# One layer of a hybrid encoder on one core: token groups of 4, 4, 3, 3, 3 tiles in place of 3, 4, 4, 3, 3

## The chip, the core and the metric

The kernel runs on one core of a Trainium2 chip. The metric is the device time of one execution in microseconds (us), as a median of several runs. The core has five engines with a queue each: PE (TensorE, matrix multiplies; its weight loads are listed as PEld), DVE (VectorE), ACT (ScalarE), POOL (GpSimd) and SP (SyncE, which here only issues transfers). An instruction waits at the head of its engine's queue until what it reads is there and what it overwrites has been used; all behind it wait too. Transfers (DMAs) are issued from SP's and ACT's queues.

## The reference

One layer is computed for 2048 new frames of one stream and 16 further frames of 8 running streams, all in float32, with 1024 channels. Cut to what matters:

```python
h = rmsnorm(x, norm_mix_pre)
P = h @ w_in            # q|k|v (3*512) | z 512 | b 4 | a 4 | B 512 | C 512 | H 512
qkv, conv_new = causal_dwconv(qkv_in, conv_prev, conv_qkv_w)   # 4 taps, then SiLU
q, k = l2norm(q) * 128 ** -0.5, l2norm(k)                      # 4 heads of 128
beta, g = sigmoid(b_raw), -exp(a_log) * softplus(a_raw + dt_bias)
o, S_new = gated_delta_rule(q, k, v, g, beta, S0, chunk)       # has a triangular solve per chunk
o = rmsnorm(o, gdn_norm_w) * silu(z)
sc_y, sc_new = causal_dwconv(sc_c * sc_h, sc_prev, conv_sc_w)  # 3 taps
x = x + rmsnorm(concat([o, sc_b * sc_y]) @ w_o, norm_mix_post)
h = rmsnorm(x, norm_ffn_pre)
x = x + rmsnorm((silu(h @ w_gate) * (h @ w_up)) @ w_down, norm_ffn_post)
```

The outputs are the new x of both streams, the last rows of both convolutions and the states S. The inputs come from one seed; some gains are multiplied by constant factors.

## The kernel before, in words

The 2176 rows are 17 tiles of 128 (tile 16 holds the running streams). Every large product is made exact enough by splitting each operand into a rounded part (`hi`, `wh`: made by a cast on ACT) and the rest (`lo`, `wl`: made by a subtraction on DVE), and by adding three products, `wh*hi + wh*lo + wl*hi`.

The kernel has four stages: the input projection with the delta rule (up to about 904 us), the output projection, the gated feed-forward part, and its way back. The change touches only the first.

**Groups and blocks.** The tiles are worked on in groups (`GROUPS`, L31). A group of n tiles is n*128 columns wide, and all 28 blocks of 128 columns of `w_in` are multiplied with it, each in 24 multiplies (8 slices of the depth, three products each, L298). `BLOCKS` names them: 0 to 3 k, 4 to 7 v, 8 to 11 q, 12 to 15 z, and from 16 on C, H, B of the short convolution. `SEQS` gives the order, one for the first group (group 0) and one for the others. Each block's weights are brought by `fetch` and `weights`, ahead of use: three buffers `w2` for the split pair, two `wr` for the raw weights. Group 0 loads raw weights (512 KB), splits them on ACT and DVE (L277, L278) and stores the pair (`wsplit`, 1024 KB) so that later groups load it ready; every fourth block is stored only in group 1. `stores` keeps a store back until the next block's load has been issued. In group 0 the rows are not yet normalised when they are multiplied; a factor per column, `rb`, is applied when a bank is taken out of PSUM (L309 and others, on DVE). In later groups the rows are scaled beforehand (`x_norm`, `x_split`).

**The written order.** PE's order is written out by hand (`tc.manual_schedule` for PE); the other engines' orders are made by a planner that simulates the program, with `tc.issue_after(i)` keeping an instruction behind `i` on the same engine. Each block takes three steps (depth slices 0 to 2, 3 to 5, 6 and 7, so 9, 9 and 6 multiplies), 84 steps a group; behind each step the functions that `events` holds for it are traced. `plan` puts them there: `PLAN` has, by number of tiles (0 stands for group 0), the steps of the gates' rates, their sums, the decays, the mask, the key norms, the key pairs, the loading of the triangular solve, its storing, the four levels that join its 32-wide answers to 128-wide ones, and the first chunk of the recurrence (a chunk a tile, six steps apart). What goes beyond step 83 runs in the next group. The solve (L578, L580) is 31 pairs of short instructions on DVE. Also in `plan`: the next group's rows are loaded and squared (`x_rows_load`, `x_rows`), their factors made and broadcast by a multiply with ones (`x_spread`, which calls `spread`: DVE sum, POOL power, DVE diagonal, PE broadcast), the transposed rows loaded, scaled and split.

**The start.** The slices of group 0 are loaded and split (L215, L216), the first block is multiplied slice by slice, then the second and third; then PE sums the squares of the rows (L888, one-column multiplies), multiplies the gates' small weights (`gate_matmuls`), and broadcasts the factors (`spread`). The fourth block can start when a PSUM bank of the first three has been taken out. Nine small inputs and constants are issued on ACT's queue after the split of the last slice (`inputs`, `late`).

Of the kernel before, what the change touches and what calls it, by code (L numbers as in the profile page):

```python
# [17 lines left out]
P = 128  # L18
D = 1024
# [11 lines left out]
GROUPS = [[0, 1, 2], [3, 4, 5, 6], [7, 8, 9, 10], [11, 12, 16], [13, 14, 15]]  # L31
# [53 lines left out]
def kernel(  # L85
# [6 lines left out]
    w_ba,  # L92
# [3 lines left out]
    conv_w,  # L96
    sc_w,
# [5 lines left out]
    gates,  # L103
    gsc,
# [25 lines left out]
    cst = const.tile([P, 904], F32, name="cst")  # L130
    half_eye = consts[:, 904:]
    nc.scalar.dma_start(out=cst[:, 0:256], in_=consts[:, 0:256])
    late = lambda: nc.scalar.dma_start(out=cst[:, 256:], in_=consts[:, 256:904])
    ident, ones, tri_p, tri_s, blk_s, smask, neg_p, neg_s = (cst[:, a:b] for a, b in CONSTS.values())
    vec = const.tile([P, 17], F32, name="vec")
    nc.scalar.dma_start(out=vec, in_=vecs)
    g_pre = vec[:, 0:8]
# [20 lines left out]
    with ExitStack() as ph:  # L158
# [18 lines left out]
        junko = gp.tile([P, P], BF16, name="junko")  # L177
        half = gp.tile([P, 4 * MAXT], F32, name="half")
# [22 lines left out]
        def spread(r, n):  # L201
            c = n * P
            rg = xbuf()
            V.tensor_mul(rg[:, :c].rearrange("p (t i) -> p t i", t=n), ident.unsqueeze(1).broadcast_to([P, n, P]),
                         r.unsqueeze(2).broadcast_to([P, n, P]))
            ps = tbank()
            T.matmul(ps[:, :c], ones, rg[:, :c], start=True, stop=True)
# [13 lines left out]
        def x_rows_load(tiles, i, nx):  # L221
            if not i:
                nx["ss"] = small.tile([P, 2 * MAXT], F32, tag="xss", name="xss")
            nx["xt"] = []
# [12 lines left out]
        def x_spread(tiles, nx):  # L237
            n = len(tiles)
            ss = nx["ss"]
            V.tensor_add(ss[:, :n], ss[:, :n], ss[:, MAXT:MAXT + n])  # L240
            nx["rb"] = spread(rstd(small, ss[:, :n], n, 1.0 / D, EPS, "x"), n)
            nx["hi"], nx["lo"], nx["xk"] = [], [], []
# [20 lines left out]
        def weights(j, gi):  # L263
# [10 lines left out]
            for q in range(parts):  # L274
                c = slice(KD // parts * q, KD // parts * (q + 1))
                wload = nc.sync.dma_start(out=wr[:, c], in_=w_in[j, :, c])
                A.copy(wh[:, c], wr[:, c])  # L277
                V.tensor_tensor(out=wl[:, c], in0=wr[:, c], in1=wh[:, c].bitcast(F32), op=ALU.subtract)  # L278
            wloads.append(wload)
            while stores:  # L280
                stores.pop()()
# [150 lines left out]
        def gate_matmuls(hi, lo, n):  # L432
            ps = bank()
            mm3(ps[:16, :n * P], [(wba[:, k, :], v[k][:, :n * P]) for k in range(KD) for v in (hi, lo)])
            return ps
# [119 lines left out]
        def solve_load(g):  # L555
# [3 lines left out]
            nc.sync.dma_start(out=Ts, in_=half_eye)  # L559
# [222 lines left out]
        def plan(g, nx, events):  # L782
# [10 lines left out]
            rates, sums, decay, mask, norms, pairs, load, store, levels, chunks = PLAN[n if gi else 0]  # L793
# [26 lines left out]
            if nx is not None:  # L820
# [5 lines left out]
                at(48 + 3 * m, x_spread, tiles, nx)  # L826
                ts = [62, 65, 68, 69, 70, 71, 72, 73]
                for k in range(KD):
                    at(ts[k], x_load, tiles, k, nx)
                    if k < NHX:  # L830
                        at(ts[k] + 3, x_norm, tiles, k, nx)
                        at(ts[k] + 4, x_split, tiles, k, nx)
                    else:
                        at(ts[k] + 4, x_norm, tiles, k, nx)
# [36 lines left out]
        for k, raw in enumerate(raws):  # L871
            sq = xbuf()
            if k % 2:
                V.tensor_mul(sq[:, :c], raw, raw)
                V.tensor_add(sq[:, :c], sq[:, :c], sqs[-1][:, :c])
                sqs[-1] = sq
            else:
                A.activation(sq[:, :c], raw, AF.Square)
# [12 lines left out]
        started = mark["hi"].ins  # L891
        inputs = ExitStack()
        inputs.enter_context(tc.issue_after(started))
        late()
        cw = gp.tile([P, 12, 4], F32, name="cw")
        scw = gp.tile([P, 4, 3], F32, name="scw")
        nc.scalar.dma_start(out=cw, in_=conv_w)
        nc.scalar.dma_start(out=scw, in_=sc_w)
        cch = gp.tile([P, 12, NS, 3], F32, name="cch")
        sch = gp.tile([P, 4, NS, 2], F32, name="sch")  # L900
        nc.scalar.dma_start(out=cch, in_=cache_c)
        nc.scalar.dma_start(out=sch, in_=cache_s)
# [4 lines left out]
        al = gp.tile([P, 4], F32, name="al")  # L907
        nega = gp.tile([P, 4], F32, name="nega")
        nc.scalar.dma_start(out=al, in_=gates[0].partition_broadcast(P))
        A.activation(nega, al, AF.Exp)  # L910
        V.tensor_scalar_mul(nega, nega, -1.0)
        gsct = gp.tile([16, 1], F32, name="gsct")
        nc.scalar.dma_start(out=gsct, in_=gsc)
        gbia = gp.tile([16, 1], F32, name="gbia")
        V.memset(gbia, 0.0)
        nc.scalar.dma_start(out=gbia[4:8, :], in_=gates[1].unsqueeze(1))
        wba_r = gp.tile([P, KD, 8], F32, name="wba_r")
        nc.scalar.dma_start(out=wba_r, in_=w_ba)
        inputs.close()
        wba = gp.tile([P, KD, 16], F32R, name="wba")  # L920
        A.copy(wba[:, :, 0:8], wba_r)
        V.tensor_sub(wba[:, :, 8:16], wba_r, wba[:, :, 0:8].bitcast(F32))
        gps = gate_matmuls(hi, lo, n)
        rb = spread(rx, n)
# [4 lines left out]
        events = {}  # L929
        for gi, tiles in enumerate(GROUPS):  # L930
            g = new_group(gi, hi, lo, rb)
# [592 lines left out]
def pack(i):  # L1524
# [13 lines left out]
    a["w_ba"] = w[:, 2048:2056].reshape(KD, P, 8).transpose(1, 0, 2)  # L1538
# [4 lines left out]
    a["conv_w"] = f["conv_qkv_w"][0].reshape(4, 12, P).transpose(2, 1, 0)  # L1543
    a["sc_w"] = f["conv_sc_w"][0].reshape(3, 4, P).transpose(2, 1, 0)
# [4 lines left out]
                                f["gdn_norm_w"][0].reshape(1, P).T], axis=1)  # L1549
    a["rows"] = np.concatenate([f["norm_mix_post"], f["norm_ffn_post"]])  # L1550
    a["gates"] = np.concatenate([f["a_log"], f["dt_bias"]])
    a["gsc"] = np.array(([-1.0] * 4 + [1.0] * 4) * 2, np.float32).reshape(16, 1)
# [33 lines left out]
```

## Time and profile before

| | |
|---|---|
| median of 3 runs | 2518.31 us (2517.99 to 2518.65) |
| the profiled execution | 2521.97 us, its span 2520.1 us |
| PE, share of the span | 98% |
| DVE, ACT, POOL | 64%, 42%, 23% |
| mean granted clock of PE | 0.992 |
| first group's block multiplies | 6.0 to 178.3 us |
| the two 512-wide groups | 178.3 to 582.0 us |
| the two last groups | 582.0 to 903.7 us |

"Busy" is the time in which an engine had at least one instruction running. Multiplies overlap, so the time that one costs is read from start to start, not from its duration. In a row of the timeline stand the start, the busy time, engine, line of the kernel, operation, output<-inputs, shapes, and in brackets the idle time before and what ended it. In the view of waits stand engine, tile and line that waited, what it waited for, then us in all, how often, and the longest. In groups of instructions stand, behind the count, the busy time, the mean in ns, and the idle time before.

### The profile page before, as it was taken

How to read it: one execution, taken by the hardware profiler on the slowest of the kernel's cores; microseconds unless marked ns; L12 is line 12 of the kernel's file. 1: busy time of each engine (PE TensorE's matmuls, PEld its weight loads, DVE VectorE, ACT ScalarE, POOL GpSimd, SP SyncE). 2: the span in 40 equal slices, each digit the busy share in tenths (PEclk: the TensorE clock that was granted, in tenths of full speed). 3: DMA queues.
4: the chain of work that ended last, by engine and by line, in shares of the span. 5: the costliest groups of instructions: out<-in, count | busy, mean ns of one | idle time of the engine just before them, and what ended most of it. 6: DMA issues, size and time to landing. Idle time of an engine off the chain costs nothing. (4 is left out here: it accounts for less than half of the span.)

```text
span 2520.1 us, 39370 instructions
## 1 busy us (share of the span) xinstructions
PE 2464.6 (98%) x14366; PEld 2253.3 (89%) x14366; DVE 1612.6 (64%) x3025; ACT 1063.8 (42%) x2355; POOL 588.1 (23%) x663
## 2 busy tenths in 40 slices
PE   8999999999999999999999999999999999999997
PEld 7988888889999988789999999999999987887786
DVE  5966645645666555868878754455555564677688
ACT  5656445445435343534444422223333345333343
POOL 1101011011010001325665400000000055455564
PEclk9999999999999999999999999999999999999999
DMA  7855555456676556669876878878998743344465
GB/s 268 320 205 193 211 194 193 176 181 225 231 243 235 196 187 223 222 227 322 293 273 239 284 246 277 268 246 262 290 308 282 255 146 121 93 126 124 129 222 184
DMA packets 282498, 561.91 MB, mean 223 GB/s; under 512 B 26108, under 2 KB 174784, under 8 KB 265024
## 3 DMA queue, kind: packets, MB, share of 16 engines
q1 hardware_dynamic: 161200, 483.52, 56.6%
q10 hardware_dynamic: 121104, 75.88, 9.6%
q8 instruction: 113, 1.85, 0.3%
q14 instruction: 81, 0.66, 0.1%
HBM read 400.62 MB, written 158.70 MB: 222 GB/s over the span
## 5 line engine op out<-in xcount | busy, mean ns | idle before, releaser
L1254 PE MATMUL fbank<-xh,fw 128*128 128x384 f32 (+1 forms) x3696 | 898.9, 326 | 4.5 <-DVE ht L1055 2.0
L298 PE MATMUL dbank<-hi,w 128*128 128x384 f32 (+1 forms) x2240 | 671.9, 368 | 8.9 <-ACT w L277 6.0
L1254 PEld LDWEIGHTS fbank<-xh,fw 128*128 128x128 f32 x3696 | 651.9, 188 | 5.8 <-ACT m L1290 2.6
L1254 PE MATMUL fbank<-xl,fw 128*128 128x384 f32 (+1 forms) x1848 | 602.5, 326 | 0.0
L298 PEld LDWEIGHTS dbank<-hi,w 128*128 128x128 f32 x2240 | 416.7, 190 | 48.2 <-ACT w L277 6.2
L1418 PE MATMUL fbank<-dw,as 128*128 128x512 f32 x1884 | 445.2, 395 | 8.0 <-DVE as L1402 2.8
L1418 PEld LDWEIGHTS fbank<-dw,as 128*128 128x128 f32 x1884 | 355.2, 189 | 91.8 <-DVE acc L1377 4.1
L298 PE MATMUL dbank<-lo,w 128*128 128x384 f32 (+1 forms) x1120 | 402.2, 359 | 1.1 <-DVE lo L216 1.1
L1254 PEld LDWEIGHTS fbank<-xl,fw 128*128 128x128 f32 x1848 | 347.4, 188 | 0.0
L1402 POOL TENSOR_TENSOR as<-ar,as 128x256 fp32r<-128x256 f32 (+1 forms) x207 | 186.4, 911 | 230.1 <-ACT as L1399 227.0
L298 PEld LDWEIGHTS dbank<-lo,w 128*128 128x128 f32 x1120 | 212.9, 190 | 18.7 <-DVE lo L216 1.6
L1377 DVE TENSOR_TENSOR acc<-acc,fbank 128x512 f32<-128x512 f32 x248 | 166.3, 682 | 97.5 <-PE fbank L1418 83.4
L1399 ACT CAST as<-ar 128x256 fp32r<-128x256 f32 (+1 forms) x288 | 118.6, 427 | 187.1 <-PE fbank L1418 133.8
L1110 POOL TENSOR_TENSOR dw<-dr,dw 128x512 fp32r<-128x512 f32 x48 | 70.2, 1473 | 521.5 <-ACT dw L1108 521.4
L1229 ACT CAST fw<-rg 128x512 fp32r<-128x512 f32 x124 | 77.3, 623 | 187.8 <-PE fbank L1254 158.9
L302 DVE SCALAR_TENSOR_TENSOR acc<-R,cw,acc 128x384 f32<-128x384 f32 (+2 forms) x180 | 121.6, 677 | 53.0 <-ACT acc L332 44.4
L1301 DVE TENSOR_TENSOR c<-u,fbank 128x384 f32<-128x384 f32 (+1 forms) x66 | 34.9, 529 | 116.0 <-PE fbank L1254 116.0
L1299 ACT ACTIVATE m<-fbank 128x384 f32<-128x384 f32 (+1 forms) x66 | 31.3, 474 | 132.8 <-PE fbank L1254 131.8
L1297 DVE TENSOR_TENSOR m<-m,m 128x384 f32<-128x384 f32 (+1 forms) x44 | 23.1, 525 | 92.1 <-ACT m L1290 92.0
L1230 POOL TENSOR_TENSOR fw<-rg,fw 128x512 fp32r<-128x512 f32 x44 | 68.6, 1558 | 45.0 <-ACT fw L1229 44.8
L324 POOL COPY hist<-R 128x3 f32<-128x3 f32 x60 | 18.3, 305 | 255.1 <-ACT R L307 202.1
L1290 ACT COPY m<-fbank 128x384 f32<-128x384 f32 (+1 forms) x66 | 30.5, 461 | 88.5 <-PE fbank L1254 57.0
(362 smaller groups left out, 3573.6 us busy)
## 6 DMA issues: line engine op xcount, KB each, us to landing
w<-wsplit SPq DMA_DIRECT2D x105, 1024.0 KB, 5.1
fw<-fsplit SPq DMA_DIRECT2D x188, 512.0 KB, 4.6
fsplit<-fw SPq DMA_DIRECT2D x94, 512.0 KB, 3.9
partd<-pt ACTq DMA_DIRECT2D x88, 384.0 KB, 6.3
rg<-in_w_gu SPq DMA_DIRECT2D x62, 512.0 KB, 3.6
wsplit<-w SPq DMA_DIRECT2D x28, 1024.0 KB, 4.9
ar<-partd SPq DMA_DIRECT2D x48, 384.0 KB, 3.3
wr<-in_w_in SPq DMA_DIRECT2D x34, 512.0 KB, 5.9
```

Of the source, the lines that this page charges most:

```text
L298: T.matmul(ps[:, :c], l[:, k, :], r[k][:, :c], start=(k == 0 and r is hi and l is wh), stop=(k == KD - 1 and l is wl))
L302: r = V.scalar_tensor_tensor(acc, raw(d), w[:, d:d + 1], acc, op0=ALU.mult, op1=ALU.add)
L1110: e.tensor_tensor(out=w[1], in0=v, in1=w[0].bitcast(F32), op=ALU.subtract)
L1229: A.copy(w[:, 0], v)
L1230: e.tensor_tensor(out=w[:, 1], in0=v, in1=w[:, 0].bitcast(F32), op=ALU.subtract)
L1254: T.matmul(ps, w_[:, c], b_[k][:, :hw], start=(first and k == 0 and ci == 0), stop=(k == KH - 1 and ci == 2), skip_group_check=not first)
L1299: A.activation(sg0, b1, AF.Silu)
L1301: V.tensor_add(c21, u2, b3)
L1377: V.tensor_add(dst, dst, ps)
L1399: ins = A.copy(a[:, 0, :n], v)
L1402: e.tensor_tensor(out=a[:, 1, :n], in0=v, in1=a[:, 0, :n].bitcast(F32), op=ALU.subtract)
L1418: T.matmul(ps, a[:, x_, q * P:(q + 1) * P], w[y_], start=(start and q == 0 and ci == 0), stop=(q == c - 1 and ci == 2), skip_group_check=True)
```

## The change

- `GROUPS` becomes 4, 4, 3, 3, 3 tiles: group 0 is 512 wide, the third 384. `PLAN` has a row for each group.
- Group 0's blocks come in another order: v between the last q blocks, and C, H, B behind them.
- `spread` is cut in two, `diagonal` and the broadcast; `x_factors` stands three steps ahead of `x_spread`.
- In the start: the squares of the rows get a buffer each and come behind the second weight block's split; five slices of the third block come before the row sums and three behind; half the gate multiplies come behind the broadcast.
- The convolution taps, the gates' weights and scalars are packed beside the gains into `vecs`, one transfer, issued first on ACT's queue. The masks (`masks`) and caches go to SP's queue, at step 9 and at step 30 of group 1. The solve's half identity is loaded behind the newest weight load.
- A weight store is issued only once more than three blocks' loads have been.

```diff
-GROUPS = [[0, 1, 2], [3, 4, 5, 6], [7, 8, 9, 10], [11, 12, 16], [13, 14, 15]]
+GROUPS = [[0, 1, 2, 3], [4, 5, 6, 7], [8, 9, 10], [11, 12, 16], [13, 14, 15]]
...
-SEQS = ([0, 12, 1, 13, 2, 14, 3, 15, 8, 16, 9, 17, 10, 18, 11, 19, 4, 20, 5, 21, 6, 7, *range(22, 28)],
+SEQS = ([0, 12, 1, 13, 2, 14, 3, 15, 8, 16, 9, 17, 10, 4, 11, 5, 18, 6, 19, 7, *range(20, 28)],
...
-PLAN = {0: (13, 18, 20, 26, 34, 35, 39, 53, (64, 67, 69, 71), 73),
-        3: (6, 12, 15, 22, 17, 27, 31, 47, (51, 54, 57, 59), 61),
-        4: (6, 12, 15, 20, 17, 24, 29, 42, (45, 48, 50, 52), 55)}
+PLAN = {0: (13, 19, 21, 25, 31, 32, 36, 49, (58, 60, 62, 64), 66),
+        1: (6, 12, 15, 20, 17, 24, 29, 42, (45, 48, 50, 52), 55),
+        2: (6, 12, 15, 22, 17, 27, 31, 47, (51, 54, 57, 59), 61),
+        3: (6, 12, 15, 22, 17, 27, 31, 47, (52, 55, 58, 60), 62),
+        4: (6, 12, 15, 22, 17, 27, 31, 47, (51, 54, 57, 59), 61)}
...
-        def x_spread(tiles, nx):
+        def x_factors(tiles, nx):
             n = len(tiles)
             ss = nx["ss"]
             V.tensor_add(ss[:, :n], ss[:, :n], ss[:, MAXT:MAXT + n])
-            nx["rb"] = spread(rstd(small, ss[:, :n], n, 1.0 / D, EPS, "x"), n)
+            nx["rg"] = diagonal(rstd(small, ss[:, :n], n, 1.0 / D, EPS, "x"), n)
+
+        def x_spread(tiles, nx):
+            nx["rb"] = spread(nx["rg"], len(tiles))
...
-            while stores:
-                stores.pop()()
+            while stores and len(wloads) > 3:
+                stores.pop(0)()
...
-            nc.sync.dma_start(out=Ts, in_=half_eye)
+            with tc.issue_after(wloads[-1].ins):
+                nc.sync.dma_start(out=Ts, in_=half_eye)
...
-                at((33 if gi else 50) + 3 * (i // 2), pair_queries, g, i)
+                at((33 if gi else 52) + 3 * (i // 2), pair_queries, g, i)
...
-                at(48 + 3 * m, x_spread, tiles, nx)
+                b = 49 + 3 * m + (0 if gi else 5)
+                at(b - 3, x_factors, tiles, nx)
+                at(b, x_spread, tiles, nx)
...
-            sq = xbuf()
             if k % 2:
-                V.tensor_mul(sq[:, :c], raw, raw)
-                V.tensor_add(sq[:, :c], sq[:, :c], sqs[-1][:, :c])
-                sqs[-1] = sq
+                sq = cp.tile([P, W1], F32, tag="cs" if k < 4 else "vraw", name="sq", bufs=2 if k < 4 else NKV)
             else:
-                A.activation(sq[:, :c], raw, AF.Square)
+                sq = xbuf()
                 sqs.append(sq)
+            with tc.issue_after(mark["cast"].ins), tc.issue_after(mark["rest"].ins):
+                if k in (1, 3):
+                    V.tensor_mul(sq[:, :c], raw, raw)
+                else:
+                    A.activation(sq[:, :c], raw, AF.Square)
+                if k % 2:
+                    squared = V.tensor_add(sqs[-1][:, :c], sqs[-1][:, :c], sq[:, :c])
...
-        for q in range(1, NPD):
-            matmuls(firsts[q], pending[q][1:], hi, lo, c, range(KD))
+        matmuls(firsts[1], pending[1][1:], hi, lo, c, range(KD))
+        matmuls(firsts[2], pending[2][1:], hi, lo, c, range(5))
...
+        rg = diagonal(rx, n)
+        matmuls(firsts[2], pending[2][1:], hi, lo, c, range(5, KD))
...
-        gps = gate_matmuls(hi, lo, n)
-        rb = spread(rx, n)
+        gps = gate_matmuls(hi, lo, n, range(0, 4))
+        rb = spread(rg, n)
+        gate_matmuls(hi, lo, n, range(4, KD), gps)
...
+        def constants():
+            with tc.issue_after(wloads[-1].ins):
+                nc.sync.dma_start(out=masks, in_=consts[:, 256:904])
+
+        events = {9: [constants]}
+
+        def caches():
+            with tc.issue_after(wloads[-1].ins):
+                nc.sync.dma_start(out=cch, in_=cache_c)
+                nc.sync.dma_start(out=sch, in_=cache_s)
```

More of the change, by code (lines that the diff above doesn't have):

```diff
@@ L128 @@
     x2d = [dram.tile([P, D], F32, name=f"x2d{t}") for t in range(NT)]
-    cst = const.tile([P, 904], F32, name="cst")
+    cst = const.tile([P, 256], F32, name="cst")
     half_eye = consts[:, 904:]
[L132 to L135, printed above, removed]
+    ident, ones = cst[:, 0:128], cst[:, 128:256]
+    vec = const.tile([P, 147], F32, name="vec")
     nc.scalar.dma_start(out=vec, in_=vecs)
+    nc.scalar.dma_start(out=cst, in_=consts[:, 0:256])
     g_pre = vec[:, 0:8]
@@ L177 @@
         junko = gp.tile([P, P], BF16, name="junko")
+        masks = gp.tile([P, 648], F32, name="masks")
+        tri_p, tri_s, blk_s, smask, neg_p, neg_s = (masks[:, a - 256:b - 256] for a, b in list(CONSTS.values())[2:])
         half = gp.tile([P, 4 * MAXT], F32, name="half")
@@ L223, in x_rows_load @@
                 nx["ss"] = small.tile([P, 2 * MAXT], F32, tag="xss", name="xss")
+                nx["hi"], nx["lo"], nx["xk"] = [], [], []
             nx["xt"] = []
@@ L430, in finish_block, with gate_matmuls @@
                     nc.scalar.dma_start(out=mixs[g["gi"]][:, h, :], in_=yo[:, :c])
-        def gate_matmuls(hi, lo, n):
-            ps = bank()
-            mm3(ps[:16, :n * P], [(wba[:, k, :], v[k][:, :n * P]) for k in range(KD) for v in (hi, lo)])
+        def gate_matmuls(hi, lo, n, ks=range(KD), ps=None):
+            ps = ps or bank()
+            for k in ks:
+                for v in (hi, lo):
+                    T.matmul(ps[:16, :n * P], wba[:, k, :], v[k][:, :n * P], start=(k == 0 and v is hi), stop=(k == KD - 1 and v is lo))
             return ps
@@ L792, in plan @@
                 at(2, gate_products, g)
-            rates, sums, decay, mask, norms, pairs, load, store, levels, chunks = PLAN[n if gi else 0]
+            rates, sums, decay, mask, norms, pairs, load, store, levels, chunks = PLAN[gi]
             at(rates, gate_rates, g)
```

78 lines of the change are left out of this document (32 added, 46 removed).

## The prediction

> **What bounds the kernel now.** The page first: which engine is full, and in which slices it is not.
>
> ```profile
> span 2520.1 us, 39370 instructions
> ...
> PE 2464.6 (98%) x14366; PEld 2253.3 (89%) x14366; DVE 1612.6 (64%) x3025; ACT 1063.8 (42%) x2355; POOL 588.1 (23%) x663
> ...
> PE   8999999999999999999999999999999999999997
> ```
>
> PE is the bound, and only what takes work or waiting from PE can count. Second view, the same engines by stage: the start, the rest of the first group, a 512-wide group (the second), the two last groups.
>
> ```profile
> 0.00:33.40 33.40, 23.96 (x115) 19.75 (x115) 16.78 (x33) 13.53 (x23) 3.89 (x13) 0.95 0.86 309
> 33.40:165.00 131.60, 122.66 (x877) 118.97 (x878) 107.11 (x234) 80.11 (x138) 14.78 (x33) 0.96 0.77 273
> 178.30:382.00 203.70, 202.57 (x1285) 169.74 (x1284) 116.92 (x271) 109.07 (x252) 20.48 (x40) 1.00 0.55 196
> 582.00:903.00 321.00, 319.33 (x2269) 307.77 (x2268) 186.11 (x502) 146.92 (x368) 32.84 (x84) 1.00 0.66 225
> ```
>
> Columns: stretch, length, busy us (and instructions) of PE, PEld, DVE, ACT, POOL, granted clock, DMA share, GB/s. PE idles 9.4 us in the start and 8.9 us in the rest of group 0, 1 to 2 us in the other two stretches; the clock is below 1 in these two stretches alone. Third, what PE waited for up to 170 us, then the slices in which the clock fell:
>
> ```profile
> PE dbank L298 <- ACT w L277: 6.0, 1, 6.0
> PE tbank L207 <- ACT w L277: 3.4, 1, 3.4
> PE gbank L600 <- DVE utd L585: 2.0, 1, 2.0
> PE gbank L639 <- DVE AU L624: 1.8, 1, 1.8
> ...
> ```
>
> ```profile
> 24.00:28.00 4.00, 4.00 (x31) 3.27 (x30) 2.36 (x5) 1.05 (x1) 0.87 (x1) 0.85 0.49 199
> 28.00:32.00 4.00, 3.68 (x14) 1.57 (x12) 1.66 (x2) 0.29 (x1) 0.00 (x0) 0.72 0.98 306
> ...
> 52.00:56.00 4.00, 4.00 (x21) 3.82 (x20) 1.14 (x3) 1.92 (x8) 0.00 (x0) 0.73 0.83 260
> ...
> 120.00:124.00 4.00, 1.47 (x3) 0.83 (x3) 3.83 (x12) 1.04 (x1) 1.03 (x1) 0.80 0.78 258
> 124.00:128.00 4.00, 4.00 (x20) 3.60 (x19) 3.59 (x14) 1.45 (x4) 0.00 (x0) 0.77 0.76 248
> ...
> 148.00:152.00 4.00, 4.00 (x35) 3.66 (x34) 0.75 (x3) 2.08 (x5) 0.18 (x1) 0.79 1.00 324
> ```
>
> A dip costs 4 x (0.15 + 0.28) = 1.7 us at 24 to 32, and 4 x (0.20 + 0.23) = 1.7 us at 120 to 128. The other two, near 52 and 148, show one of their two slices here and are taken at the same 1.7 us: four dips, 6.8 us.
>
> The Trainium skill (TensorE: Matmul & The Clock Gate, Part 1) says that the clock halves only after about a whole idle window of 3.4 us. Only the wait of 3.4 us would reach that; the dip at 52, behind a wait of 1.8 us, is against it, so the trace decides. Taken at its word, the dips at 24, 52 and 148 would have another cause than the waits, which is the first rival below.
>
> **The change: work that is only moved.** Before, groups of 3, 4, 4, 3, 3 tiles; after, 4, 4, 3, 3, 3. Two groups are 512 wide and three 384 wide in both, 28 blocks of 24 multiplies each. Nothing is saved in PE's width; block time moves from the third group to the first:
>
> ```profile
> 17.20 0.33 PE L298 MATMUL dbank<-lo,w 128*128 128x384 f32 x1
> ...
> 17.72 0.33 PE L298 MATMUL dbank<-lo,w 128*128 128x384 f32 x1
> ...
> 193.90 0.39 PE L298 MATMUL dbank<-lo,w 128*128 128x512 f32 x1
> ...
> 194.58 0.39 PE L298 MATMUL dbank<-lo,w 128*128 128x512 f32 x1
> ```
>
> A `lo` multiply and the two `hi` ones behind it take 0.52 us at 384 and 0.68 us at 512: 173 and 227 ns each, 4.15 and 5.45 us a block. A step (a third of a block, 8 multiplies) is 1.38 and 1.82 us.
>
> **A, the start (to the fourth block).**
>
> ```profile
> 11.27 0.84 PE L298 MATMUL dbank<-hi,w 128*128 128x384 f32 x2
> ...
> 11.91 0.52 PE L298 MATMUL dbank<-lo,w 128*128 128x384 f32 x1
> ...
> 17.15 0.53 ACT L878 ACTIVATE xk<-AU 128x384 f32<-128x384 f32 x1 [4.36 <-DMA gsct<-in_gsc]
> ...
> 23.87 2.80 PE L888 MATMUL tbank<-cst,xk 128*128 128x1 f32 x24
> ...
> 30.87 0.81 PE L207 MATMUL tbank<-xk,cst 128*128 128x384 f32 x2
> ...
> 33.40 0.41 PE L298 MATMUL dbank<-hi,w 128*128 128x384 f32 x1 [1.72 <-DVE R L309]
> ```
>
> The first multiplies run at 0.32 us each (two from 11.27, the next at 11.91), half speed; at 512 that is 0.32 x 4/3 = 0.43. After: first multiply at 6.2 (6.0 before, with 64 KB more ahead of it); half speed for 15 multiplies (6.4, to about 12.6); the other 57 of three blocks x 0.227 = 13.0, to 25.6; row sums 32 instead of 24, 2.8 x 4/3 = 3.7; 16 gate multiplies at the block rate 3.6; the broadcast 0.81 x 4/3 = 1.1: 34.0. I add 0.5 for a dip that may stay. The wait of 1.72 for the first bank's evacuation gets half the gate multiplies as cover, 8 x 0.227 = 1.8, so it goes; without that cover it costs its 1.7 again. The gap of 4.36 on ACT, behind small inputs issued one by one, goes with the packing and lets the third block's weights come in time. So 34.5, against 33.4 plus the moved work, 88 multiplies x 0.054 = 4.8: 3.7 us gained. Ends: -1 (the first tiles are 2 MB instead of 1.5, 1.6 us more at the stretch's 309 GB/s, and the waits stay) to 4.9 (no dip, first multiply at 5.6).
>
> Stores of the first three weight blocks now go behind the fourth load.
>
> ```profile
> wsplit<-w SPq DMA_DIRECT2D x28, 1024.0 KB, 4.9
> ```
>
> The fourth cast waits for the first store (three buffers), and the fifth load stands behind all three on SP's queue. A store lands 4.9 us after its issue: begun near 15, one after another, the third ends near 30 and the load behind it lands near 36; PE wants that block at 34.5 + 5.45 = 39.9. Cost nothing; if the cover is gone, at most one block, 5.5.
>
> The 324 KB of masks and 176 KB of caches change to SP's queue, at steps 9 and (group 1) 30; wanted ten steps (18 us) and a group later: nothing. The half identity for the solve is no longer loaded at 8.65 us but at its step, behind a weight load. It has the copies and the transpose before the solve as cover (5 + 2 us); if late, DVE waits 2 us and that falls under D.
>
> **B, the gate sums.** `gate_sums` stands 6 steps behind `gate_rates` instead of 5, and steps are longer: 48 x 0.227 = 10.9 us of PE work for 40 x 0.173 = 6.9. The chain between them took some 9 us:
>
> ```profile
> 41.19 0.35 PE L452 MATMUL gbank<-cst,xk 16*128 16x16 f32 x3
> ...
> 50.25 0.39 PE L481 MATMUL gbank<-gg,cst 128*128 128x12 f32 x2 [1.75 <-DVE gg L473]
> ```
>
> Wait 1.75 and its dip 1.7 go: 3.4 (ends 0 and 3.5).
>
> **C, factors of the next group's rows.** DVE sums, POOL's power, DVE's diagonal and PE's broadcast were one step; now the broadcast stands 3 steps later, 5.45 us in group 0:
>
> ```profile
> 119.64 0.15 DVE L240 TENSOR_TENSOR xss<-xss 128x4 f32<-128x4 f32 x1
> ...
> 121.69 0.69 DVE L204 TENSOR_TENSOR xk<-cst,xr 128x512 f32<-128x512 f32 x1
> ...
> 122.53 2.04 PE L207 MATMUL tbank<-xk,cst 128*128 128x512 f32 x2 [3.40 <-ACT w L277]
> ...
> 682.20 0.91 PE L207 MATMUL tbank<-xk,cst 128*128 128x384 f32 x2 [1.05 <-DVE xk L204]
> ```
>
> The chain is 122.4 - 119.6 = 2.8 us, so the wait of 3.40 and its dip go, 5.1 (ends 0 and 5.1), and in the fourth group 1.05, where three steps are 4.2 us. Late next: the norms for group 1, moved from step 65 to 69 and still eight steps before they are needed.
>
> **D, the triangular solve in group 0.** From `solve_load` to `level_a` there were 25 steps, now 22, and beside them stand blocks q, v, q, v, B, v, C for B, q, C, v, H, v, B, v.
>
> ```profile
> 86.00:133.30 47.30, 41.90 (x244) 40.11 (x244) 44.75 (x113) 27.88 (x54) 5.78 (x12) 0.96 0.83 303
> ```
>
> ```profile
> L278 DVE TENSOR_TENSOR w<-wr,w 128x1024 fp32r<-128x1024 f32 x9 | 11.0, 1219 | 1.3 <-ACT w L277 1.3
> ...
> L569 DVE STREAM_TRANSPOSE As<-pk 128x1024 f32<-128x1024 f32 x1 | 2.1, 2117 | 0.2 <-ACT pk L567 0.2
> ```
>
> ```profile
> 86.00:133.30 47.30, 7.76 (x31) 0.96 0.83 303
> ```
>
> ```profile
> L302 DVE SCALAR_TENSOR_TENSOR acc<-R,cw,acc 128x512 f32<-128x512 f32 x72 | 54.0, 750 | 41.8 <-ACT acc L332 40.4 <-issue 0.2
> L302 DVE SCALAR_TENSOR_TENSOR acc<-R,cw,acc 128x384 f32<-128x384 f32 x72 | 43.8, 612 | 7.1 <-ACT acc L332 3.9 <-ACT acc L334 2.5
> ```
>
> DVE is busy 44.75 of 47.3 us: 11.0 are weight splits, 15.6 the solve (62 instructions; the third row is one half of them, L578, the other half is taken as equal), about 3.8 three transposes (the first 2.1, the two of the answer estimated at 1.7), and 14.3 work that grows with the columns (a tap takes 612 ns at 384, 750 at 512: x 1.23). After: 8 splits 9.8 + 15.6 + 3.8 + 17.6 = 46.8, with the same 2.5 of idle 49.3. PE: before 45.3 to `level_a`, less wait 3.4 and dip 1.7, is 40.2 = 200 x 0.173 + 5.6; after 176 x 0.227 + 5.6 x 4/3 = 47.4. DVE is late by 1.9 us, as it was by 2.0. So nothing is gained: 0 (ends +5.5, both waits 2.0 and 1.8 and a dip gone, and -26, the last rival).
>
> **Sum.** A 3.7 + B 3.4 + C 5.1 + 1.05 + D 0 = 13.3 us. The profiled execution took 2521.97 us, 1.9 outside its span and 3.7 above the median of 2518.31; against it the sum gives 2508.7, against the median **2505.0 us**, which is the forecast.
>
> **Rivals.**
> 1. The waits go, the dips stay: the first dip stands behind no long wait but beside one-column and 16-row multiplies. B and C lose 1.7 each and A another 1.2: 2509.6. For it: the 24 one-column multiplies at 23.87. Against: three dips of four beside waits. By the rule of the Trainium skill above (TensorE: Matmul & The Clock Gate, Part 1), C's dip alone would go, which gives 2505.0 + 1.7 + 1.2 = 2507.9.
> 2. It does not do what it says: DVE, busy 95% beside the solve, is later at `level_a` by about 12 us and eats the gain: 2518. For it: v blocks, three taps each, are drawn beside the solve. Against: in D the splits and the solve do not grow with the columns.
> 3. Slower, by the same backlog: it decides from a wait of about 20 us at `level_a` (2.0 + 13.3 + 5). If the whole stretch of 47.3 grew by half, to 71, PE at 47.4 would wait 24, 22 more than before, with two more dips 25.4: 2518.3 - 13.3 + 25.4 = 2530. For it: solve steps alternate on DVE, each behind other work. Against: the 512-wide second group, DVE busy 117 of 204 us, shows no wait there.
>
> **How the numbers follow.** Forecast 0.52, rival 1 0.19, rival 2 0.13, rival 3 0.16. Forecast alone: 2499 to 2512, from the ends of A to C. The range 2497 (A 4.9, B 3.5, C 6.1, D 5.5, together 20, and 1 for small gaps elsewhere) to 2520 takes in rival 2 and leaves out rival 3 and little else. A measurement here tells 0.2%, 5 us, from no change. Faster 0.71, same 0.13, slower 0.16.
>
> **What would show it.** A: the fourth block's first multiply near 34, no wait before it. B: no wait at `gate_sums`, clock 1 there. C: no wait at the broadcast in groups 0 and 3. D: about 2 us at `level_a` near 115 to 125. Third group near 160 us long, like the last two. Wrong if `level_a` or the fifth block's weights make PE wait over 5 us, or if the last 1600 us, which this change does not touch, move.

## The result, and the profile after

The changed kernel takes **2525.78 us** (median of 10 runs, 2521.06 to 2531.63), the kernel before 2518.62 us (10 runs, 2517.21 to 2522.37) beside it: ratio 1.0025, 95% interval 1.0017 to 1.0034 (ratios here are those on record with the runs; the two medians alone give 1.0028). It is slower by about a quarter of a per cent; 2505.0 us was forecast, with 2497 to 2520 as the range. The profiled execution took 2528.28 us.

The page of the changed kernel, its span and its engines, is nearly that of before:

```profile
span 2526.5 us, 39364 instructions
...
PE 2464.5 (98%) x14374; PEld 2252.8 (89%) x14374; DVE 1615.1 (64%) x3022; ACT 1059.5 (42%) x2353; POOL 600.9 (24%) x663
```

PE is busy for the same 2464.5 us in a span 6.4 us longer: the work did not grow, PE stands still for longer. The stages show where. First the changed kernel (start to the fourth block, rest of group 0, third group, the last two groups; the columns are those of the prediction), then the kernel before for its third group, which the prediction did not show:

```profile
0.00:37.80 37.80, 31.21 (x123) 23.16 (x123) 19.28 (x31) 16.83 (x26) 3.70 (x12) 0.91 0.91 327
37.80:165.00 127.20, 121.44 (x775) 101.26 (x776) 99.64 (x206) 76.77 (x121) 16.29 (x30) 0.96 0.60 209
426.00:582.60 156.60, 152.98 (x1108) 147.89 (x1107) 85.49 (x228) 77.03 (x185) 17.06 (x40) 1.00 0.64 226
582.60:912.50 329.90, 322.57 (x2270) 309.70 (x2269) 186.61 (x506) 149.25 (x372) 34.05 (x85) 0.99 0.61 216
```

```profile
383.70:582.00 198.30, 198.30 (x1246) 166.00 (x1245) 105.34 (x253) 93.56 (x210) 18.64 (x41) 1.00 0.53 183
```

Before, PE had no idle time in the third group and 1.7 us in the last two (the row of 582 to 903 in the prediction); now it idles 3.6 and 7.3 us there, in groups for which the prediction had no new waits. The table has the length of each group, from the start of its first block multiply to that of the next group's (the last one: to the end of its last block multiply):

```
us                        before   changed   expected by the prediction's steps
first block multiply         6.0       6.3   6.2
fourth block                33.4      37.8   34.5
rest of group 0            144.9     183.0
second group (512 wide)    205.4     205.2   as before
third group                198.3     156.6   near 160
fourth group               163.5     168.9   1.05 less
fifth group                158.1     161.3   as before
```

What PE waits for, grouped, in groups 3 to 5 and the first microseconds behind them (420 to 915 us): the changed kernel, then the kernel before (420 to 906). The columns are total us, times, longest.

```profile
PE tbank L347 <- ACT qT L340: 6.7, 6, 2.3
PE gbank L624 <- ACT xs L610: 2.3, 3, 1.1
PE dbank L1045 <- DVE wol L1010: 1.0, 1, 1.0
PE gbank L715 <- DVE st L776: 1.0, 1, 1.0
PE tbank L347 <- ACT kT L340: 0.8, 2, 0.6
```

```profile
PE dbank L1031 <- ACT mh L986: 1.3, 1, 1.3
PE tbank L207 <- DVE xk L204: 1.0, 1, 1.0
PE gbank L600 <- DVE utd L585: 0.4, 1, 0.4
```

The first and the last row of the changed kernel, 7.5 us in eight waits, are of a kind that the kernel before does not have: PE has come to the transposes of a finished q or k block (`turned`, L347) before ScalarE's SiLU (L340) has made their input. In group 0 the waits of the changed kernel (0 to 220 us) behind the first weights' load are these:

```profile
...
PE gbank L607 <- issue: 3.7, 1, 3.7
PE gbank L551 <- DVE AU L552: 2.0, 1, 2.0
...
```

The waits at `gate_sums` and at the broadcast of the row factors are gone, as forecast; one at `pair_keys` (L551) is new, and that at `level_a` (L607) has grown from 2.0 to 3.7 us.

### The profile page after: what moved, and what is told of

It is laid out like the page before. It is cut to its first block, busy times and chain, and to the rows that moved or that the text cites. A ratio compares the mean times of both kernels' runs of the same rounds, so it can differ in the third digit from the quotient of the medians.

```text
span 2526.5 us, 39364 instructions
## 1 busy us (share of the span) xinstructions
PE 2464.5 (98%) x14374; PEld 2252.8 (89%) x14374; DVE 1615.1 (64%) x3022; ACT 1059.5 (42%) x2353; POOL 600.9 (24%) x663
## 5 line engine op out<-in xcount | busy, mean ns | idle before, releaser
L306 DVE SCALAR_TENSOR_TENSOR acc<-R,vec,acc 128x512 f32<-128x512 f32 (+2 forms) x180 | 121.4, 676 | 52.1 <-ACT acc L336 45.2
L328 POOL COPY hist<-R 128x3 f32<-128x3 f32 x60 | 23.7, 395 | 249.7 <-ACT R L311 201.4
```

The source lines that it names most:

```text
L306: r = V.scalar_tensor_tensor(acc, raw(d), w[:, d:d + 1], acc, op0=ALU.mult, op1=ALU.add)
```

## The experiments

**First lot: which part of the change loses the time.** The first kernel is the changed one with the fourth group's levels and chunks at the steps they had before:

```diff
-        3: (6, 12, 15, 22, 17, 27, 31, 47, (52, 55, 58, 60), 62),
+        3: (6, 12, 15, 22, 17, 27, 31, 47, (51, 54, 57, 59), 61),
```

> The changed kernel (2525.8 us) with one row of its plan put back: the fourth group's levels at 51, 54, 57, 59 and first chunk at 61 instead of 52, 55, 58, 60 and 62. Theory 'step': the one-step shift of the fourth group delays its work into the fifth, which lost 3.2 us, and its own end; then the two last groups take 163.5 and 158 us as before instead of 168.9 and 161, and the time falls by 5 to 8 us to 2518 to 2521. Theory 'order': the losses of the groups 3 to 5 (PE waiting at the transposes of q for ACT's SiLU) come from the order that the planner gave DVE and ACT, not from this row; then within 2 us of 2525.8.

Measured: 2520.20 us against 2521.71 of before, 0.9997 (0.9986 to 1.0008). The waits at the transposes stay, 6.7 us in six here:

```profile
PE tbank L347 <- ACT qT L340: 6.1, 5, 2.3
...
PE tbank L347 <- ACT kT L340: 0.6, 1, 0.6
```

So the shift of one step costs some 7 us in this company (1.0025 to 0.9997), but it is not what brings the waits.

The second kernel is the one before with the new groups, order and steps alone:

```diff
-GROUPS = [[0, 1, 2], [3, 4, 5, 6], [7, 8, 9, 10], [11, 12, 16], [13, 14, 15]]
+GROUPS = [[0, 1, 2, 3], [4, 5, 6, 7], [8, 9, 10], [11, 12, 16], [13, 14, 15]]
...
-            rates, sums, decay, mask, norms, pairs, load, store, levels, chunks = PLAN[n if gi else 0]
+            rates, sums, decay, mask, norms, pairs, load, store, levels, chunks = PLAN[gi]
...
-                at((33 if gi else 50) + 3 * (i // 2), pair_queries, g, i)
+                at((33 if gi else 52) + 3 * (i // 2), pair_queries, g, i)
```

(with the five rows of `PLAN` and the first row of `SEQS` as the change has them). The third is the changed kernel with the old groups, order and steps, so all the rest of the change alone.

> The kernel before with the groups of 4, 4, 3, 3, 3 tiles, the new block order and the new plan rows alone; small inputs, squares, stores, the broadcast in one step and the half identity as before. If the regrouping carries the losses of the last three groups: their sum with the third stays at 486 us and the time is 2524 to 2530, worse than the changed kernel's 2525.8 by what the start and the cut broadcast gained (5 to 8 us) if those gained anything. If the other parts carry them: 2512 to 2519.

> The changed kernel with groups of 3, 4, 4, 3, 3 tiles, the block order and the plan rows of before: packed inputs, squares, cut broadcast, late stores, late half identity alone. If the regrouping carries the losses, these parts keep what was forecast for them (start 3.7, broadcast 5.1 and 1.05): 2508 to 2514. If these parts carry the losses: 2519 to 2526, with PE waiting at the transposes of q in the last groups.

Measured: the regrouping alone 2526.91 us, 1.0023 (1.0014 to 1.0032); the rest alone 2515.27 us, 0.9980 (0.9971 to 0.9989). All the loss is in the regrouping. The two do not add: 1.0023 and 0.9980 would make 1.0003, and the changed kernel is at 1.0025, so most of what the rest gains alone is not gained beside the regrouping; why was not tried.

Alone, the rest of the change gains 5 us. Its profile is that of its slowest run (2519.10 us), 2.9 us shorter than that of before: 2.4 are gained in the start and 1.4 in the fourth group, and 0.9 are lost in the other stages. Group 0 behind the start gains nothing there: from the fourth block to the end of the group it takes 145.4 us (31.0 to 176.4) for 144.9 before. Its two largest waits, and two slices around the longest (the clock is the third column from the end):

```profile
PE gbank L605 <- issue: 9.9, 1, 9.9
PE dbank L300 <- ACT w L279: 6.6, 2, 6.2
```

```profile
120.00:128.00 8.00, 1.28 (x8) 0.96 (x6) 7.29 (x22) 2.11 (x5) 2.76 (x2) 0.72 0.84 295
128.00:136.00 8.00, 4.81 (x59) 4.78 (x60) 4.05 (x12) 4.75 (x9) 0.59 (x2) 0.50 0.10 37
```

Of the waits of 1.75 and 3.40 us, 0.2 is left, and `level_a` (L605 there) now waits 9.91 us and starts at 131.19, where it started at 133.26 before. PE came 10 us earlier (121.28 for 131.26), the solve ended 2 us earlier, no more than the fourth block's own start (31.0 for 33.4): what was freed in front of it was waited off behind it.

The fourth kernel tests the row sums: of the 32 one-column multiplies only the last 8 are done (`for k, sq in enumerate(sqs[3:])`), so the row factors miss three quarters of the squares.

> The changed kernel with 8 of its 32 one-column multiplies for the row sums of the first group (the other three of four buffers of squares are left out of the sums, so the rows' factors are not the reference's). In the changed kernel they run from 23.96 to 28.6 us and the clock is halved from about 27 to 33.8. If they bring the dip: they take 0.9 us, the clock stays at 1 up to 34 us, and the fourth block starts 6 to 7 us earlier, at 31 to 32 us. If the small gate multiplies or something else brings it: 2.7 to 3.5 us earlier, with the dip still there.

Measured: 2521.08 us, 1.0003 (0.9992 to 1.0014), the fourth block at 31.7 us for 37.8. Of the 6.1 us, 3.7 are the multiplies (32 in 4.64 us, 8 in 0.95), the rest is the slow clock, which is gone (1.00 in 24 to 32 us). But 37.8 is the latest start of this kind that was seen: the five other profiles of the same start have 35.2 to 35.5, and against these 3.5 to 3.8 us are gained.

**Second lot: why PE is early at the transposes.** Laid beside that of before, PE's order in the fourth group has changed: the transposes stand a third of a block, one step, ahead of their old place. The line that places them is the same in both kernels, so the diff does not show it:

```
                        if later:
                            wait = 10 - n if gi else 7 if BLOCKS[j][0] == "v" else 13
                            events.setdefault(3 * slot + wait, []).insert(0, later)
```

`n` here is not the size of the group at hand. It is set once, ahead of the loop, to the size of the FIRST group. With three tiles there the wait was 7 steps in groups 1 to 4; with four it is 6. Two kernels follow: the changed one with a 7 written in place of `10 - n`, and the one before with a 6. The other two hold the shift of the fourth group against it: 7 and the old steps together, and the shift alone in the kernel before.

```diff
-                            wait = 10 - n if gi else 7 if BLOCKS[j][0] == "v" else 13
+                            wait = 7 if gi else 7 if BLOCKS[j][0] == "v" else 13
```

> One number in the changed kernel: the wait of the k and q blocks' transposes, `10 - n` steps behind their block in groups 1 to 4, is written as 7. `n` there is the size of the FIRST group, so the regrouping made it 6 where it was 7, in a line that the diff does not show. Theory 'n': the eight PE waits of the changed kernel in front of these transposes in the three 384-wide groups (0.68, 1.48, 0.60, 0.21, 2.30, 0.16, 0.52, 1.47: 7.4 us) go, and the slow clock behind the one of 2.30; fourth and fifth group again near 165 and 159 us (168.9 and 161 in the changed kernel); the time falls by 6 to 9 us, to 2517 to 2520. Rival 'order' (VectorE's and ScalarE's instructions of these groups are placed in another order, the decay masks between the taps of the q blocks): the waits fall by less than half, 2523 to 2526.

> The kernel before with the transposes' wait written as 6 in groups 1 to 4, nothing else. Theory 'n': the waits at the q transposes appear in the two 384-wide groups (fourth and fifth, about 3.1 and 2.2 us, and one slow stretch of 1.7) and not in the two 512-wide ones, whose steps are 1.82 us instead of 1.38: 5 to 7 us slower, 2523 to 2526. Rival 'order': VectorE's order of before stays as it is, no such waits, within 1 us of 2518.6.

> The changed kernel with both: the transposes' wait written as 7, and the fourth group's levels and chunks at their old steps (51, 54, 57, 59 and 61). Theory 'n': the two causes lie at different places (the transposes near 25 to 50 us of a group, the levels at its end), so the gains add: 5 from the one and 6 to 9 from the other, 2512 to 2515. Rival 'order': the same as with the old steps alone, 2519 to 2521. A third way: both gains are one and the same slack, so that the second brings nothing on top of the first: 2517 to 2520.

> The kernel before with the fourth group's levels and chunks one step later (52, 55, 58, 60 and 62), as the changed kernel has them, and nothing else; the fifth group keeps its steps. If the shift costs by itself: 3 to 6 us slower, the fourth group 2 to 4 us longer than its 163.5, the rest in the fifth, 2522 to 2524. If it cost only in the company of the transposes' waits: within 1 us of 2518.6.

Measured, against 2520.36 us of the kernel before, run beside them:

```
                                    us        ratio   interval
changed, wait 7                     2515.72   0.9981  0.9972 to 0.9989
before, wait 6                      2526.22   1.0023  1.0014 to 1.0031
changed, wait 7, old fourth steps   2512.55   0.9970  0.9958 to 0.9982
before, fourth steps shifted        2520.10   1.0000  0.9991 to 1.0009
```

The one number accounts for the loss, in both directions. Put back, it takes 0.44% (11 us) off the changed kernel, which is then faster than before; put alone into the kernel before, it costs 0.23%, as much as the whole regrouping did (1.0023). PE's waits from 420 us to the end of the fifth group: the changed kernel with 7, then the kernel before with 6.

```profile
...
PE gbank L624 <- ACT xs L610: 0.6, 2, 0.5
PE tbank L347 <- ACT qT L340: 0.2, 1, 0.2
```

```profile
PE tbank L343 <- ACT qT L336: 3.9, 3, 2.3
PE tbank L343 <- ACT kT L336: 0.6, 1, 0.6
...
```

With 7, third, fourth and fifth group take 152.1, 163.7 and 159.0 us (156.6, 168.9 and 161.3 with 6), 12.0 us less. Of these, 7.3 are the transposes' waits, 1.7 the waits at L624 (2.3 and 0.6) and 1.7 the slow clock behind the longest wait; the other 1.3 are not accounted for. Why a step matters there: the longest of the waits, in the changed kernel's timeline (start, length, engine, line; in brackets the idle time), PE first, then DVE and ACT, which make its input.

```profile
629.86 0.34 PE L302 MATMUL dbank<-hi,w 128*128 128x384 f32 x1
632.49 0.55 PE L347 MATMUL tbank<-cst,qT 128*128 128x128 f32 x3 [2.30 <-ACT qT L340]
```

```profile
628.83 0.63 DVE L306 SCALAR_TENSOR_TENSOR acc<-R,vec,acc 128x408 f32<-128x408 f32 x1
629.54 1.90 DVE L535 TENSOR_TENSOR dt<-dt,c 128x512 f32<-128x512 f32 x3
631.36 0.63 DVE L306 SCALAR_TENSOR_TENSOR acc<-R,vec,acc 128x408 f32<-128x408 f32 x1
```

```profile
632.02 0.42 ACT L340 ACTIVATE qT<-acc 128x256 f32<-128x256 f32 x1 [0.71 <-DVE acc L306]
```

```profile
632.00:636.00 4.00, 3.51 (x22) 3.51 (x23) 1.90 (x6) 1.11 (x3) 0.19 (x1) 0.74 0.11 43
636.00:640.00 4.00, 4.00 (x21) 4.00 (x20) 0.27 (x1) 0.49 (x1) 0.00 (x0) 0.83 0.00 0
```

The three taps of the q block (L306; the second and third are shown) run on VectorE with the decay scale (L535, 1.90 us) between the second and the third, and SiLU follows the last. The same place in the kernel with 7, on PE:

```profile
621.82 1.95 PE L551 MATMUL gbank<-kT 128*128 128x128 f32 x16
...
625.44 0.55 PE L347 MATMUL tbank<-cst,qT 128*128 128x128 f32 x3
```

One step is more than its 1.38 us of block multiplies here. `insert(0, later)` puts the transposes in front of what else stands at their step: with 6 they come ahead of the 16 multiplies of `pair_keys` (L551), with 7 they come one step later and behind them, 3.6 us later (621.82 to 625.44). Even so there was no slack: with 7 PE is ready at 625.34 and the SiLU ends at 625.39. VectorE has the decay scale between the same two taps in both kernels (at 622.50 with 7), so it was PE's order that changed the wait. The waits of 1.48 and 1.47 us in the third and fifth group stand in front of `pair_keys` too. The wait of 2.30 us is followed by two slices at 0.74 and 0.83, another 4 x (0.26 + 0.17) = 1.7 us. In the second group, where a step is 1.82 us, none of the five kernels with a wait of 6 steps has one.

The shift of the fourth group alone costs nothing (1.0000), where 3 to 6 us were expected if it cost by itself; with the 7 in place undoing it gains 2.8 us, which the intervals do not tell from nothing. Only beside the early transposes did it cost 7. Why the two together cost more than their sum was not tried.

**Third lot: the solve in group 0, and the slow clock of the start.** All four start from the changed kernel with 7 and the old fourth steps (0.9970). The first has group 0's levels and chunks three steps later, the second in addition the key pairs and the solve one step later:

```diff
-PLAN = {0: (13, 19, 21, 25, 31, 32, 36, 49, (58, 60, 62, 64), 66),
+PLAN = {0: (13, 19, 21, 25, 31, 32, 36, 49, (61, 63, 65, 67), 69),
...
+PLAN = {0: (13, 19, 21, 25, 31, 33, 37, 50, (61, 63, 65, 67), 69),
```

> The changed kernel with the transposes' wait of 7 and the fourth group's old steps (2512.55 by itself, 0.9970 of before), and the first group's four levels and its chunks three steps later (61, 63, 65, 67 and 69 for 58, 60, 62, 64 and 66; a step is 1.82 us there). In the kernel without this edit PE waits 4.50 us at level_a (149.59), because VectorE ends the solve and its two transposes only then, and two slices of 8 us behind it show a clock of 0.72 and 0.85 (3.4 us). Theory 'the solve is late at its step': VectorE's end does not move, PE does other blocks meanwhile; wait and slow clock go, 6 to 8 us less, 2504.5 to 2506.5. Rival 'VectorE is the bound of the stretch': PE then runs ahead of VectorE and stands at another of its results (bank, tap, query pairs), and at most 2 us are gained: 2510.5 to 2513.

> As the one before, and the first group's key pairs one step later (33 for 32, the solve's load 37 for 36, its store 50 for 49). Without it PE waits 2.72 us at pair_keys (92.28) and the clock is 0.81 in the 8 us there (1.5 us). If that wait is a matter of the step: 0.9 us of it stay and the slow clock goes, 3 us less than the run before it, 2501.5 to 2503.5. If VectorE's backlog sets it: the later load makes the solve later by 1.8 us, which the levels at 61 no longer cover in full, and nothing is gained against the run before.

Measured: 2509.25 us, 0.9958 (0.9945 to 0.9971), and 2507.64 us, 0.9955 (0.9943 to 0.9968), against 2518.72 of before. `level_a` without the edit, then with the levels three steps later:

```profile
149.59 1.92 PE L607 MATMUL gbank<-utd,AU 32*32 32x32 f32 x64 [4.50 <-issue]
```

```profile
152.07 1.20 PE L607 MATMUL gbank<-utd,AU 32*32 32x32 f32 x64 [2.09 <-issue]
```

Three steps are 5.45 us; the wait shrank by 2.4 and the solve itself ended 2.5 us later, since VectorE was given other work meanwhile. The profiles' group 0 behind the start is 178.4 us for 184.2, more than the waits explain; part of it is a slow clock behind `level_a` that lasts 3.4 us for 6.8. Neither theory alone: about half of the room was gained at `level_a` and half went to VectorE, which hardly rests there (kernel without the edit, 104 to 144 us; the third busy time is VectorE's):

```profile
104.00:144.00 40.00, 40.00 (x203) 33.69 (x202) 37.29 (x89) 22.55 (x47) 6.82 (x11) 1.00 0.69 244
```

The second kernel's pair wait is gone, but the `level_a` wait is 3.6 us again. Both are faster than the kernel before by 10 to 11 us; from each other and from 0.9970 the intervals hardly tell them. The second is the fastest seen.

The other two have the row sums in four lots of 8, one behind each of the third block's first four depth slices, alone and together with the second edit above:

```diff
-        matmuls(firsts[2], pending[2][1:], hi, lo, c, range(5))
         psn = tbank()
         for k, sq in enumerate(sqs):
+            matmuls(firsts[2], pending[2][1:], hi, lo, c, [k])
...
-        matmuls(firsts[2], pending[2][1:], hi, lo, c, range(5, KD))
+        matmuls(firsts[2], pending[2][1:], hi, lo, c, range(4, KD))
```

> The changed kernel with the transposes' wait of 7 and the fourth group's old steps, and the 32 one-column multiplies of the row sums in four lots of 8, one behind each of the first four depth slices of the third block, not in one run; the same multiplies, the same sums. In the kernel without this edit they take 3.5 us in a row (23.25 to 26.74), and the multiplies behind them run at half speed (0.57 in 28 to 32). If the slow clock comes from PE's array standing nearly empty for 3.5 us: it goes, the fourth block starts 1.7 us earlier, near 33.7 for 35.45, 2510.5 to 2511.5. If it comes from one-column multiplies as such, however placed: 35 to 36 again, 2512 to 2513.

> All of these edits together: transposes' wait 7, fourth group's old steps, first group's levels at 61 and chunks at 69, pairs at 33, solve's load at 37 and store at 50, row sums in four lots. If the gains are those of the runs above and add: 4.5 + 3.4 + 2.7 + 1.7 = 12 us at most below 2512.55, 2500 to 2503. If VectorE bounds the stretch of the solve, an earlier start of the fourth block only lengthens the waits there: 2507 to 2511.

Measured: 2512.65 us, 0.9973 (0.9962 to 0.9983), and 2508.84 us, 0.9959 (0.9946 to 0.9971): no gain. One run of sums, then four lots, in the slice behind the sums and at the fourth block:

```profile
28.00:32.00 4.00, 4.00 (x12) 1.99 (x11) 1.99 (x3) 0.28 (x2) 1.02 (x1) 0.57 1.02 394
...
35.45 0.47 PE L302 MATMUL dbank<-hi,w 128*128 128x512 f32 x1 [0.25 <-DVE R L313]
```

```profile
28.00:32.00 4.00, 4.00 (x18) 2.37 (x17) 1.83 (x2) 0.38 (x2) 0.35 (x1) 1.00 0.97 377
...
35.48 0.47 PE L302 MATMUL dbank<-hi,w 128*128 128x512 f32 x1 [0.99 <-DVE R L313]
```

The slow clock is gone, yet the fourth block starts at the same time: PE now waits for the first bank's evacuation (L313). VectorE takes that up no earlier, because a weight split stands before it; first one run of sums, then four lots:

```profile
32.86 1.23 DVE L282 TENSOR_TENSOR w<-wr,w 128x1024 fp32r<-128x1024 f32 x1 [1.64 <-ACT w L281]
...
34.62 0.68 DVE L313 TENSOR_TENSOR R<-dbank,rb 128x512 f32<-128x512 f32 x1
```

```profile
32.91 1.23 DVE L282 TENSOR_TENSOR w<-wr,w 128x1024 fp32r<-128x1024 f32 x1 [2.84 <-ACT w L281]
...
34.65 0.68 DVE L313 TENSOR_TENSOR R<-dbank,rb 128x512 f32<-128x512 f32 x1
```

The split waits for ScalarE's cast of the same weights, which begins at 31.78 and 31.83. The row factors' broadcast is not what holds it: with four lots it comes 0.7 us earlier (31.61 for 32.34). The slow clock had been covering this. Whether the evacuation ahead of the split would gain the time was not tried.

## Why the prediction was wrong

**The step that failed is the count of the change itself.** "28 blocks of 24 multiplies each" in both kernels and a cost of nothing for the groups behind the first took it that only the steps written in the diff move. A step that the diff does not show, the transposes' wait in groups 1 to 4, follows from the size of the first group and moved by one. That is 11 us, and it alone turns the sign: without it the changed kernel is at 0.9981, 4.8 us faster than before, inside the forecast's range.

**The sum.** Even so, 13.3 us were forecast and 4.8 came. By steps, in the kernel with the wait of 7:

- A, the start. 34.5 us forecast, 37.8 in the changed kernel's profile, but 35.2 to 35.5 in the five other profiles that have the same start. Against 33.4 + 4.8 of moved work 35.4 is a gain of 2.8 for 3.7. The wait for the first bank went as forecast (0.25 us is left), the 32 row sums took 3.6 for 3.7; what was mis-sized is the slow clock behind them, put at 0.5 and measured at 1.7 (0.57 in one slice). But without that slow clock (the four lots above) the block starts at 35.48 too, behind a wait of 0.99: the cover for the first bank's evacuation was too short as well, because the sum had no term for the weight split that VectorE does before it. These gains are known to about 1 us: the start of the kernel before ended at 32.0 and 34.0 us in the two other profiles that have it.
- B and C. No wait at `gate_sums` nor at either broadcast, nor slow clock there: right as to the waits, 8.5 us with their dips. As to the time, wrong: the rest alone of the change shows, in its profile, the same waits gone and group 0 behind the start as long as before, with 9.9 us at `level_a`.
- D. PE's path from `solve_load` to `level_a` was right: 47.4 us forecast; 48.0 (98.7 to 146.7) in the changed kernel and 47.4 with the wait of 7. VectorE's was too short: 46.8 busy and "the same 2.5 of idle" made 49.3. The same stretch, to the end of VectorE's solve, in the changed kernel and in the one with 7:

```profile
98.70:150.40 51.70, 48.00 (x242) 40.07 (x240) 45.34 (x109) 30.22 (x58) 7.02 (x12) 0.99 0.65 226
```

```profile
95.30:147.80 52.50, 47.39 (x239) 39.60 (x238) 45.95 (x111) 30.11 (x58) 7.01 (x12) 1.00 0.65 225
```

Busy 45.3 and 46.0, a little under the forecast, but idle 6.4 and 6.6. Most of the new idle time is one wait, for ScalarE's copies of the packed pairs, which in turn wait for VectorE's last pair product. The changed kernel, VectorE and then ScalarE:

```profile
103.26 2.12 DVE L576 STREAM_TRANSPOSE As<-pk 128x1024 f32<-128x1024 f32 x1 [3.91 <-ACT pk L574]
```

```profile
98.73 4.50 ACT L574 COPY pk<-AU 32x512 f32<-32x512 f32 x4 [2.37 <-DVE AU L552]
```

Before, VectorE waited 0.2 us for these copies (the row of L569 in the prediction). And the pair products themselves are a new wait for PE, of 2.0 us (L551), which no step of the prediction had. The waits of the kernel with 7 in group 0, and its clock behind `level_a`:

```profile
PE gbank L607 <- issue: 5.1, 1, 5.1
PE gbank L551 <- DVE AU L552: 1.9, 1, 1.9
```

```profile
148.00:152.00 4.00, 4.00 (x70) 3.45 (x68) 0.47 (x1) 3.92 (x7) 0.52 (x1) 0.50 0.14 54
152.00:156.00 4.00, 4.00 (x63) 2.98 (x63) 2.84 (x4) 2.36 (x4) 0.18 (x1) 0.68 0.08 31
```

  Rest of group 0 and third group together take 335.3 us there, for 343.2 before; 4.8 of that is the work moved to the start, so B to D gained 3.1 of 8.5. The rows give about that: 8.5, less 3.1 more at `level_a` (5.1 for 2.0) and 1.9 at `pair_keys`, less 1.6 more of slow clock (4 x (0.50 + 0.32) = 3.3 for 1.7), and the old wait of 1.8 behind `level_a` gone, is 3.7.
- C in the fourth group: its 1.05 us wait is gone; the group is 163.7 us for 163.5.

**The rivals.** Rival 2 ("DVE, busy 95% beside the solve, is later at `level_a` by about 12 us and eats the gain") has the place and the engine right; it was priced at 12 us and took some 5, and not by VectorE's own work but by what it waits for. Rival 3 had the sign, but by luck and not the place: no wait near 20 us came at `level_a`. Rival 1 was right for the start only: the dip beside the one-column multiplies stayed, those of `gate_sums` and the broadcast went with their waits. None of the three named the transposes.

**What was to show it.** The third group is below 160 us and the tail is 1613.7 us for 1616.5, both as forecast; the 5 us for `level_a` that would make the forecast wrong were passed in some of the kernels, not in the changed one. None of these tests took the length of the fourth and fifth group, where much of the loss was.

## What to carry to other kernels

When a constant changes, look for every expression that reads it, also outside the diff, and compare the order of the instructions of one engine before and after in a stretch that "does not change": here transposes that came one step early cost 11 us. A wait taken away in front of a point where another engine's chain sets the time is only moved to that point; price it by the end of that chain, idle time in it included, before counting the gain.

## What was not expected of the hardware

Runs of one-column multiplies were followed by a halved clock though PE did not wait. In the changed kernel, the row sums and the clock of the three slices around them:

```profile
23.96 4.64 PE L901 MATMUL tbank<-cst,xk 128*128 128x1 f32 x32
```

```profile
24.00:28.00 4.00, 4.00 (x31) 4.00 (x30) 0.14 (x1) 1.04 (x1) 0.00 (x0) 0.79 1.00 393
28.00:32.00 4.00, 4.00 (x11) 3.25 (x12) 1.85 (x3) 0.00 (x0) 1.03 (x1) 0.50 1.00 406
32.00:36.00 4.00, 4.00 (x15) 1.61 (x14) 1.23 (x1) 1.35 (x2) 0.00 (x0) 0.85 0.67 236
```

Here the slow stretch is worth 4 x (0.21 + 0.50 + 0.15) = 3.4 us, in the five other profiles of the same start 1.7: which of the two comes varies from run to run. All seven profiles with 32 in a row show a slow stretch behind them. With eight, or with four lots of eight and three wide ones between, the clock stayed at 1.00 (three profiles). The 24 of the kernel before do not decide it: two profiles of its start show the slow clock, a third (the fourth group's steps shifted) has 1.00 from 20 to 40 us. And a wait of 2.30 us was followed by 1.7 us of slow clock (the slices from 632 on, above), but not always: of the five profiles that have this wait (2.27 to 2.30 us), three show it (the changed kernel, the one with 8 row sums, the kernel before with 6), and two keep 1.00 (the old fourth steps, the regrouping alone). The Trainium skill (TensorE: Matmul & The Clock Gate, Part 1) asks for a whole idle window of about 3.4 us. The run of one-column multiplies fits it if such multiplies count as idle, which no run here shows directly, and the wait of 2.30 us does not fit it where the slow clock came.
